# The first adaLN modulation of a two-layer trunk: condition against weights, or weights against condition, on TensorE

## The chip, the core and the metric

The kernel runs on one core of one Trainium2 chip. The metric is device microseconds (us) of one execution, from which medians are taken. The core has five engines with an instruction stream each: TensorE (PE, matrix products, with a separate weight load PEld), VectorE (DVE), ScalarE (ACT), GpSimd (POOL) and SyncE (SP, which here issues most DMAs). Every engine works through its stream in order and waits on semaphores for the others.

## The reference

Two layers over a sequence of 512 tokens of width 1024, in float32. Every sub-layer begins with an RMS norm that is modulated by a shift and a scale, which come from a condition vector c of width 1024:

```python
cond = jax.nn.silu(c)
for layer in range(DEPTH):
    mod = cond @ ada_w[layer] + ada_b[layer]
    shift_m, scale_m, gate_m, shift_f, scale_f, gate_f = jnp.split(mod, N_MOD, axis=-1)
    h = modulate(rms_norm(x, norm_mix_g[layer]), shift_m, scale_m)   # h * (1 + scale) + shift
    ...
    z = h @ ev_w_in[e]           # layer 0: u for S5, then hq, hf, hi, hg for HGRN2
```

Layer 0 is an S5 state space on the 512 channels u beside an HGRN2 recurrence, layer 1 a gated linear attention, and each is followed by a SwiGLU of hidden width 2816. This document is about the start: shift_m and scale_m of layer 0, 2048 numbers, each a sum over 1024 products of cond with a column of ada_w, then h, then the product h @ ev_w_in that gives u.

## The kernel before

Activations stand with channels on the 128 partitions, in eight blocks of 128 channels by 512 tokens (xT[m], and h as a pair hhi, hlo of rounded value and rest, in float32r). A large product is three products of such halves (lines 275 to 277: hi by hi, hi by lo, lo by hi). The helper wsplit makes a weight's halves, ACT the rounded one, DVE the rest.

**The first modulation.** ada_first_loads(half) issues on SP the loads of sixteen weight tiles of 128x512 (256 KB): eight blocks k of the 1024 input channels, for i = 1 (scale) and i = 0 (shift), for half of the output channels. They go into sixteen slots with the tag "s" and one with "n"; a tile of the second half takes the slot of a tile of the first when that has been read. ada_first(half, ws, rows, n) then computes both sums. The scale is done on DVE: acc = acc + w * cond[k] over all 128x512 elements (line 116). The shift is done on PE for the first n blocks, with one column of cond as the weights that stand and the tile of 512 columns passing (line 405), which gives one row of 512 numbers; the rest, for the second half where n = 4, also on DVE (acs). At the end the partitions are summed and turned into columns by products with ones (lines 416 to 421), the bias is added, and gsc, the gain (1 + scale) * norm_mix_g, is formed (line 425). Both halves have their own gsc, and the normed blocks m = 0 to 3 (norm_out, with the tiles ht and hlo) wait for the first, m = 4 to 7 for the second.

**Around it.** s5_params, some 90 small DVE and ACT steps on 128x16 tiles, is put ahead of everything by a priority. x is turned by PE through the identity, four transposes of 128x128 for each block into the PSUM tile xps, and copied by ACT to xT. xn, x times its inverse RMS, is turned likewise into xnps; blocks 4 to 7 are copied to xnT, since they wait longer. Four PSUM tiles rotate under the tag "mm" (xps, xnps 0 to 3, u) and two each under "a" and "b". u has four output blocks q, each of eight input blocks k: u_part does k = 0 to 3, the last loop k = 4 to 7. s5_in_out, s5_mats and s5_tables give POOL its work (B and C matrices, the W products, rotation tables cos and ph).

**What sets the order.** The tile framework schedules the instructions of each engine by its own estimate of time, within dependencies, and fixes the order when the program is built. after(ins) makes what is issued inside it come after ins; "hold" is a POOL copy of gsc that POOL's later work is put behind.

Of the kernel before, what the change touches and what calls it, by code (L numbers as in the profile page):

```python
# [41 lines left out]
def trunk(  # L42
# [22 lines left out]
    def tt(name, tag, shape=(P, T), dtype=F32):  # L65
        return tp.tile(list(shape), dtype, tag=tag, name=name, bufs=SLOTS[tag])
# [4 lines left out]
    def const(name, shape, dtype=F32):  # L71
        return cp.tile(list(shape), dtype, name=name, tag=name)
# [4 lines left out]
    def ps_a(name, shape=(P, T)):  # L77
        return pa.tile(list(shape), F32, tag="a", name=name)
# [6 lines left out]
    def act(o, i, f, **kw):  # L85
        return A.activation(out=o, in_=i, func=f, **kw)  # L86
# [19 lines left out]
    def ttv(e, o, a, b, op):  # L106
        e.tensor_tensor(out=o, in0=a, in1=b, op=op)  # L107

    def tsv(e, o, a, s1, op0, s2=None, op1=None):
        if s2 is None:  # L110
            e.tensor_scalar(out=o, in0=a, scalar1=s1, scalar2=None, op0=op0)
        else:
            e.tensor_scalar(out=o, in0=a, scalar1=s1, scalar2=s2, op0=op0, op1=op1)

    def stt(o, a, s, b, op0, op1):
        V.scalar_tensor_tensor(out=o, in0=a, scalar=s, in1=b, op0=op0, op1=op1)  # L116
# [21 lines left out]

    prow = tt("prow", "s", (16, 4, P))
    nc.scalar.dma_start(out=prow[:, 0, :], in_=s5_lam_re[0].rearrange("(j g) p -> j (g p)", g=2))  # L140
    nc.scalar.dma_start(out=prow[:, 1, :], in_=s5_lam_im[0].rearrange("(j g) p -> j (g p)", g=2))
    lsrow = const("lsrow", [16, 2])
    nc.scalar.dma_start(out=lsrow, in_=s5_log_step[0].rearrange("(j g) -> j g", g=2))
# [211 lines left out]
    def norm_out(xn, parts, q, l, base, m):  # L355

        hh, hl = parts[m]
        gain, shift = gsc[:, q, m : m + 1], mod[:, l, base + m : base + m + 1]
        act(hh, xn, AF.Identity, scale=gain, bias=shift)
        t = tt(f"ht{l}{m}", "t")  # L360
        stt(t, xn, gain, hh.bitcast(F32), ALU.mult, ALU.subtract)
        return V.tensor_scalar(out=hl, in0=t, scalar1=shift, scalar2=None, op0=ALU.add)
# [14 lines left out]
    def ada_first_loads(half):  # L377
        tags = iter("s" * 15 + "n")
        ws = []
        for k in range(KT):  # L380
            for i in (1, 0):
                w = tt(f"ar0{i}{half}{k}", next(tags))
                nc.sync.dma_start(out=w, in_=ada_w[0, k * P : (k + 1) * P, i * D + half * T : i * D + half * T + T])
                ws.append(w)
        return ws
# [4 lines left out]
    def ada_first(half, ws, rows=(), n=KT):  # L390


        acc = tt(f"acc01{half}", "sc")
        acs = tt(f"acc00{half}", "X") if n < KT else None
        fp = ps_a(f"row{half}")
        row = fp[0:1, :]
        last = None
        for k in range(KT):
            c_ = cond[:, k : k + 1]
            if k == 0:  # L400
                tsv(V, acc, ws[0], c_, ALU.mult)
            else:
                stt(acc, ws[2 * k], c_, acc, ALU.mult, ALU.add)
            if k < n:
                ins = PE.matmul(row, lhsT=c_, rhs=ws[2 * k + 1], start=(k == 0), stop=(k == n - 1))
            elif k == n:
                tsv(V, acs, ws[2 * k + 1], c_, ALU.mult)
            else:
                stt(acs, ws[2 * k + 1], c_, acs, ALU.mult, ALU.add)
            if k + 1 in rows:  # L410
                last = rows[k + 1](ins)
        rsb = tt(f"rsb{half}", "sc")[0:1, :]
        act(rsb, row, AF.Copy)
        with after(last):
            for m in range(4):
                PE.matmul(fp[:, m : m + 1], lhsT=acc[:, m * P : (m + 1) * P], rhs=ones[:, 0:1], start=True, stop=True)
            for m in range(4):
                o = fp[:, 4 + m : 5 + m]
                ins = PE.matmul(o, lhsT=rsb[:, m * P : (m + 1) * P], rhs=ones[0:1, 0:1], start=True, stop=acs is None)
                if acs is not None:  # L420
                    ins = PE.matmul(o, lhsT=acs[:, m * P : (m + 1) * P], rhs=ones[:, 0:1], start=False, stop=True)
        for i in range(2):
            c0 = i * 8 + half * 4
            ttv(V, mod[:, 0, c0 : c0 + 4], fp[:, 4 - 4 * i : 8 - 4 * i], cols1[:, c0 : c0 + 4], ALU.add)
        V.scalar_tensor_tensor(
            out=gsc[:, 0, half * 4 : half * 4 + 4], in0=mod[:, 0, 8 + half * 4 : 12 + half * 4], scalar=1.0,
            in1=cols1[:, 96 + half * 4 : 100 + half * 4], op0=ALU.add, op1=ALU.mult)
        return ins
# [139 lines left out]
    def s5_params():  # L568
# [37 lines left out]
        tact(ch, t1, AF.Sin, scale=-0.5, bias=hpic)  # L606
        ttv(V, sb, sh, ch, ALU.mult)
# [41 lines left out]
        return L, cr, ci, rho, fh, fl, pc  # L649
# [272 lines left out]
    with tc.high_priority(offset=-3000):  # L922
        prm = s5_params()
# [5 lines left out]
    aw.append(ada_first_loads(1))  # L929
    raw.append(wraw(us[2], KT, "u2"))  # L930
    crow = tt("crow", "n", (32, 2, P))
# [4 lines left out]
    bcl = s5_in_out_loads()  # L936
    ada_first(0, aw[0])
    hold = G.tensor_copy(out=sm("hold", [P, 4]), in_=gsc[:, 0, 0:4])
# [6 lines left out]
    for m in range(KT):  # L945
        ps = mm_ps(f"xps{m}")
        for b in range(NB):
            PE.transpose(ps[:, b * P : (b + 1) * P], xtok[b][:, m * P : (m + 1) * P], ident)
        act(xT[m], ps, AF.Copy)
    for b in range(NB):  # L950
        if b % 2:
            act(xn[:, b, :], xtok[b], AF.Copy, scale=xrs[:, b : b + 1])
        else:
            tsv(V, xn[:, b, :], xtok[b], xrs[:, b : b + 1], ALU.mult)
    h = norm_parts("m0")
    xns = []
    for m in range(KT):
        ps = (mm_ps if m < 4 else ps_b)(f"xnps{m}")
        for b in range(NB):
            PE.transpose(ps[:, b * P : (b + 1) * P], xn[:, b, m * P : (m + 1) * P], ident)  # L960
        if m < 4:
            hl = norm_out(ps, h, 0, 0, 0, m)
        else:
            xns.append(tt(f"xnT{m}", "t"))
            act(xns[-1], ps, AF.Copy)
    ups = [mm_ps(f"u{q}") for q in range(4)]
    wu = [blocks(wsplit(raw[q], KT, f"u{q}")) for q in range(2)]
# [9 lines left out]
    with after(hl):  # L977
        fold1 = ada_first(1, aw[1], {4: u_part(0, range(4))}, 4)
    raw.append(wraw(us[3], KT, "u3"))
    with after(hl):  # L980
        wu.append(blocks(wsplit(raw[2], KT, "u2")))
    for q in range(1, 3):
        u_part(q, range(4))(None)
    for m in second:
        norm_out(xns[m - 4], h, 0, 0, 0, m)
# [6 lines left out]
    for n in (2, 4):  # L992
        PE.transpose(tps[:, 8 * n : 16 * n], crow[n].rearrange("k g p -> k (g p)"), ident[0 : 8 * n, 0 : 8 * n])
        tact(conds[n], tps[:, 8 * n : 16 * n], AF.Silu)
# [4 lines left out]
    with after(hold):  # L999
        mats = [s5_mats(0)]  # L1000
    with after(G.tensor_copy(out=sm("hold", [P, 4]), in_=gsc[:, 0, 4:8])):
        rot = [s5_tables(q) for q in range(4)]
# [258 lines left out]
```

## Time and profile before

| | us |
|---|---|
| median of 3 runs (1344.96 to 1350.41) | 1345.29 |
| the profiled execution | 1345.65 |
| its span, first to last instruction | 1343.9 |
| PE busy (matmul records) | 1280.0 |
| DVE busy | 766.8 |
| ACT busy | 514.1 |
| POOL busy | 141.4 |

Busy times are of single engines and overlap. A busy PE is not PE at its peak: its level of clock is a separate column (PEclk), and a record lasts longer at the lower level. In a timeline each row is a run of like instructions on one engine: start, duration of the run, line, tiles written and read, shapes, count, and in brackets the idle time before it with what ended it. PE shows two records for one float32 product, and one for a float32r product or a transpose.

### The profile page before, as it was taken

The numbers are of one execution on the slowest core, as the hardware profiler recorded it, in microseconds if no ns is written. First come the engines' busy times: TensorE is split into PE (matmuls) and PEld (weight loads), VectorE is DVE, ScalarE is ACT, GpSimd is POOL, SyncE is SP. The second block draws the span as 40 slices with busy tenths as digits, with TensorE's granted clock in tenths as the row PEclk, the third lists the DMA queues.
The fourth block names the chain that finished last, engine by engine and source line by source line (L and its number), as shares of the span: only waits on it lengthen the run. The fifth ranks groups of instructions, "written<-read, shape, count | busy, mean of one in ns | idle before, by whom it ended". The sixth has DMA issues, their size and how long they took to land.

```text
span 1343.9 us, 18265 instructions
## 1 busy us (share of the span) xinstructions
PE 1280.0 (95%) x6949; PEld 1097.6 (82%) x6949; DVE 766.8 (57%) x1433; ACT 514.1 (38%) x939; POOL 141.4 (11%) x148
## 2 busy tenths in 40 slices
PE   7797999899999999999999999999899999999997
PEld 3577887778888888888888999997888888888886
DVE  5786995787765566566356446657743333333344
ACT  5477358534522222232244433433432222222322
POOL 0593451110100000000010000000100000000000
PEclk9798998999999999999999999999799999999999
DMA  9742531633097669996250322114033323333232
GB/s 305 173 126 79 157 110 38 152 98 102 20 223 189 186 183 230 205 219 185 74 157 21 102 65 78 56 48 133 17 98 103 97 71 99 113 99 104 65 92 79
DMA packets 222824, 159.69 MB, mean 119 GB/s; under 512 B 16752, under 2 KB 195248, under 8 KB 222736
## 3 DMA queue, kind: packets, MB, share of 16 engines
q1 hardware_dynamic: 221696, 157.48, 43.3%
q8 instruction: 54, 0.88, 0.3%
q10 hardware_dynamic: 1040, 1.05, 0.3%
q14 instruction: 34, 0.28, 0.1%
HBM read 156.40 MB, written 2.10 MB: 118 GB/s over the span
## 4 chain that ended last, share of the span: by engine, by line
PE 81%; DVE 10%; ACT 3%; DMA 3%; issue 2%; SPq 0%; POOL 0%; DVEq 0%; ACTq 0%
PE f L275 18%; PE f L276 18%; PE f L277 18%; DMA ar<-in_ada_w_dram 2%; PE op L276 2%; PE lv_g L465 2%; PE op L277 2%; PE op L275 2%; ACT yf L86 1%; PE gr L300 1%; PE gr L301 1%; PE gv L301 1%; PE gr L299 1%; PE gv L300 1%; PE gv L299 1%
## 5 line engine op out<-in xcount | busy, mean ns | idle before, releaser
L276 PE MATMUL f<-hlo_f,whi_f 128*128 128x512 f32 (+1 forms) x736 | 280.8, 383 | 0.4 <-DVE hlo_f L116 0.4
L275 PE MATMUL f<-hhi_f,whi_f 128*128 128x512 f32 (+1 forms) x736 | 279.9, 383 | 0.9 <-ACT hhi_f L86 0.9
L277 PE MATMUL f<-hhi_f,wlo_f 128*128 128x512 f32 (+1 forms) x736 | 280.1, 382 | 0.0
L86 ACT ACTIVATE whi_f<-raw_f 128x1024 fp32r<-128x1024 f32 x88 | 93.3, 1061 | 309.3 <-PE f L276 167.4
L107 DVE TENSOR_TENSOR wlo_f<-raw_f,whi_f 128x1024 fp32r<-128x1024 f32 x88 | 107.7, 1224 | 113.9 <-ACT whi_f L86 113.2
L276 PEld LDWEIGHTS f<-hlo_f,whi_f 128*128 128x128 f32 x736 | 139.2, 189 | 27.2 <-DVE hlo_f L116 1.4
L275 PEld LDWEIGHTS f<-hhi_f,whi_f 128*128 128x128 f32 x736 | 138.9, 190 | 27.5 <-ACT hhi_f L86 1.4
L277 PEld LDWEIGHTS f<-hhi_f,wlo_f 128*128 128x128 f32 x736 | 139.3, 189 | 26.4
L204 DVE SCALAR_TENSOR_TENSOR acc<-ar,cond,acc 128x512 f32<-128x512 f32 x154 | 122.9, 798 | 39.9 <-DMA ar<-in_ada_w_dram 37.8
L277 PE MATMUL f<-hi_g,wlo_c 128*128 128x512 f32 x312 | 121.8, 390 | 0.0
L276 PE MATMUL f<-lo_g,whi_c 128*128 128x512 f32 x312 | 121.7, 390 | 0.0
L275 PE MATMUL f<-hi_g,whi_c 128*128 128x512 f32 x312 | 121.3, 390 | 0.0
L86 ACT ACTIVATE whi_c<-raw_c 128x768 fp32r<-128x768 f32 (+1 forms) x56 | 44.8, 801 | 161.9 <-PE f L276 107.7
L107 DVE TENSOR_TENSOR g<-g,f 128x512 f32<-128x512 f32 x44 | 30.2, 687 | 106.1 <-PE f L277 106.0
L107 DVE TENSOR_TENSOR wlo_c<-raw_c,whi_c 128x768 fp32r<-128x768 f32 (+1 forms) x56 | 50.3, 898 | 60.6 <-ACT whi_c L86 59.1
L275 PEld LDWEIGHTS f<-hi_g,whi_c 128*128 128x128 f32 x312 | 58.6, 188 | 12.1
L276 PEld LDWEIGHTS f<-lo_g,whi_c 128*128 128x128 f32 x312 | 58.6, 188 | 12.1
L277 PEld LDWEIGHTS f<-hi_g,wlo_c 128*128 128x128 f32 x312 | 58.6, 188 | 12.0
L116 DVE SCALAR_TENSOR_TENSOR x<-f,mod,x 128x512 f32<-128x512 f32 (+1 forms) x36 | 24.8, 689 | 40.5 <-PE f L277 40.4
L107 POOL TENSOR_TENSOR na_m<-na_m,nsq_m 128x256 f32<-128x256 f32 x7 | 5.9, 856 | 361.7 <-ACT nsq_m L86 361.7
L300 PE MATMUL gv<-wlo_gv,hhi_m 128*128 128x256 f32 x128 | 36.7, 287 | 0.0
L301 PE MATMUL gv<-whi_gv,hlo_m 128*128 128x256 f32 x128 | 36.6, 287 | 0.0
(668 smaller groups left out, 2651.8 us busy)
## 6 DMA issues: line engine op xcount, KB each, us to landing
raw_f<-in_ffn_w_dram SPq DMA_DIRECT2D x88, 512.0 KB, 4.0
ar<-in_ada_w_dram SPq DMA_DIRECT2D x256, 128.0 KB, 4.2
ar<-in_ada_w_dram SPq DMA_DIRECT2D x64, 256.0 KB, 5.4
raw_c<-in_ffn_w_dram SPq DMA_DIRECT2D x32, 384.0 KB, 3.5
raw_c<-in_ffn_w_dram SPq DMA_DIRECT2D x24, 320.0 KB, 3.2
raw_gv<-in_od_w_in_dram SPq DMA_DIRECT2D x8, 512.0 KB, 3.7
raw_gr<-in_od_w_in_dram SPq DMA_DIRECT2D x8, 512.0 KB, 4.5
raw_o<-in_ev_w_out_dram SPq DMA_DIRECT2D x8, 384.0 KB
```

Of the source, the lines that this page charges most:

```text
L86: return A.activation(out=o, in_=i, func=f, **kw)
L107: e.tensor_tensor(out=o, in0=a, in1=b, op=op)
L116: V.scalar_tensor_tensor(out=o, in0=a, scalar=s, in1=b, op0=op0, op1=op1)
L204: ins = V.scalar_tensor_tensor(out=acc, in0=w, scalar=c_, in1=acc, op0=ALU.mult, op1=ALU.add)
L275: PE.matmul(ps, lhsT=hi, rhs=ah[:, ts], start=(i == 0), stop=False)
L276: PE.matmul(ps, lhsT=hi, rhs=al[:, ts], start=False, stop=False)
L277: ins = PE.matmul(ps, lhsT=lo, rhs=ah[:, ts], start=False, stop=(i == n - 1))
L299: PE.matmul(o, lhsT=ah[:, s], rhs=hi, start=(k == 0), stop=False)
L300: PE.matmul(o, lhsT=ah[:, s], rhs=lo, start=False, stop=False)
L301: PE.matmul(o, lhsT=al[:, s], rhs=hi, start=False, stop=(k == KT - 1))
L465: PE.matmul(ps[0:nk, w, :].rearrange("p (n b) -> p n b", b=b), lhsT=K[:, w * P : w * P + nk], rhs=qv[:, w * nb : (w + 1) * nb, b:], start= ...
```

## The change

ada_first now computes both sums on PE in the other arrangement: a block of 128x128 of the weight tile stands, one column of cond passes, and the 128 sums come out as a column of PSUM, accumulated over k. Per half that is a product of the identity with the bias columns, then 64 products (eight k, two i, four m), one copy to mod and gsc. The DVE sums, the row, its copy (rsb) and the folds with ones go. Between the products, at given k, the argument rows puts other PE work:

```diff
+    def ada_first(half, ws, rows=()):
+        fp = ps_a(f"row{half}")[:, 0:8]
+        m4 = slice(half * 4, half * 4 + 4)
+        bias, mods = (t.rearrange("p (i m) -> p i m", m=8)[:, :, m4] for t in (cols1[:, 0:16], mod[:, 0, 0:16]))
+        f2 = fp.rearrange("p (i m) -> p i m", m=4)
         last = None
+        PE.matmul(fp, lhsT=ident, rhs=bias, start=True, stop=False)
         for k in range(KT):
-            c_ = cond[:, k : k + 1]
-            if k == 0:
-                tsv(V, acc, ws[0], c_, ALU.mult)
-            else:
-                stt(acc, ws[2 * k], c_, acc, ALU.mult, ALU.add)
-            if k < n:
-                ins = PE.matmul(row, lhsT=c_, rhs=ws[2 * k + 1], start=(k == 0), stop=(k == n - 1))
...
+            for i in (1, 0):
+                for m in range(4):
+                    with after(last):
+                        ins = PE.matmul(f2[:, i, m : m + 1], lhsT=ws[2 * k + 1 - i][:, m * P : (m + 1) * P],
+                                        rhs=cond[:, k : k + 1], start=False, stop=(k == KT - 1 and i == 0 and m == 3))
             if k + 1 in rows:
                 last = rows[k + 1](ins)
-        rsb = tt(f"rsb{half}", "sc")[0:1, :]
-        act(rsb, row, AF.Copy)
...
+        V.tensor_copy(out=mods, in_=f2)
...
-    with tc.high_priority(offset=-3000):
-        prm = s5_params()
+    prm = s5_params()
+    next(prm)
...
-    aw.append(ada_first_loads(1))
+    aw.append(ada_first_loads(1, range(4)))
     raw.append(wraw(us[2], KT, "u2"))
+    bcl = s5_in_out_loads()
+    aw[1] += ada_first_loads(1, range(4, KT))
...
+    turn_x(*range(4))(None)
+    last = ada_first(0, aw[0], {4: turn_x(4, 5), 5: turn_x(6, 7), 7: turn_xn(*range(4))})
+    turn_xn(*range(4, KT))(last)
...
+    for m in range(4):
+        with after(hl):
+            hl = norm_out(xnp[m], h, 0, 0, 0, m)[1]
+        if m % 2:
+            with after(hl):
+                wu.append(blocks(wsplit(raw[m // 2], KT, f"u{m // 2}")))
+    with after(hl):
+        prm = next(prm)
...
     with after(hl):
-        fold1 = ada_first(1, aw[1], {4: u_part(0, range(4))}, 4)
+        wu.append(blocks(wsplit(raw[2], KT, "u2")))
+    fold1 = ada_first(1, aw[1], {2 * q + 2: u_part(q, range(4)) for q in range(3)})
...
-    with after(hold):
+    with after(hold), after(ins[0]):
         mats = [s5_mats(0)]
-    with after(G.tensor_copy(out=sm("hold", [P, 4]), in_=gsc[:, 0, 4:8])):
+    with after(G.tensor_copy(out=sm("hold", [P, 4]), in_=gsc[:, 0, 4:8])), after(ins[0]), after(ins[1]):
         rot = [s5_tables(q) for q in range(4)]
```

s5_params has become a generator: its first part, up to the sines, is issued at the start, the rest after the fourth normed block. The log-step row is loaded ahead of the two parameter rows on ACT's queue. In the second half of the program's start, ins is the pair of ACT's and DVE's last steps of normed block 7, which the W products and the tables now come after.

On PE, in the first half, before (row is the PSUM row of the sums, xps the turned x, xnps the turned xn):

```order
L174 MATMUL tps<-cs,rows_91 128x128
L405 MATMUL row_348<-ar_264,cond 1x512
L405 MATMUL row_348<-ar_268,cond 1x512
L948 MATMUL xps_425<-cs,xin 128x128 x4
L948 MATMUL xps_431<-cs,xin 128x128 x4
L405 MATMUL row_348<-ar_272,cond 1x512
L948 MATMUL xps_437<-cs,xin 128x128 x4
L948 MATMUL xps_443<-cs,xin 128x128 x4
L405 MATMUL row_348<-ar_276,cond 1x512
L405 MATMUL row_348<-ar_280,cond 1x512
```

One row product of 512 columns for each block k stands between the transposes. In the same place now:

```order
L403 MATMUL row_340<-cond,ar_218 128x1 x4
L403 MATMUL row_340<-cond,ar_220 128x1 x4
L937 MATMUL xps_374<-cs,xin 128x128 x4
L937 MATMUL xps_380<-cs,xin 128x128 x4
L403 MATMUL row_340<-cond,ar_222 128x1 x4
L403 MATMUL row_340<-cond,ar_224 128x1 x4
L937 MATMUL xps_394<-cs,xin 128x128 x4
L937 MATMUL xps_400<-cs,xin 128x128 x4
L403 MATMUL row_340<-cond,ar_226 128x1 x4
L403 MATMUL row_340<-cond,ar_228 128x1 x4
L403 MATMUL row_340<-cond,ar_230 128x1 x4
L403 MATMUL row_340<-cond,ar_232 128x1 x4
```

Every weight tile, of both sums, has four products of one column; 32 products precede the first of these transposes.

On PE again, ahead of the second gsc, before: the end of the u products of blocks 0 to 3, transposes of the S5 C matrices (cps), and the folds.

```order
L276 MATMUL u_521<-hlo_m_454,whi_u_581 128x512
L277 MATMUL u_521<-hhi_m_453,wlo_u_583 128x512
L679 MATMUL cps_661<-cs,cn 128x128 x4
L679 MATMUL cps_668<-cs,cn 128x128 x4
L416 MATMUL row_533<-ones,acc_531 128x1 x4
L419 MATMUL row_533<-ones,rsb_562 128x1
L421 MATMUL row_533<-ones,acc_532 128x1
```

Now, between the u products of output block 1 and those of output block 2:

```order
L276 MATMUL u_565<-hlo_m_474,whi_u_504 128x512
L277 MATMUL u_565<-hhi_m_474,wlo_u_506 128x512
L403 MATMUL row_572<-cond,ar_268 128x1 x4
L403 MATMUL row_572<-cond,ar_270 128x1 x4
L403 MATMUL row_572<-cond,ar_272 128x1 x4
L403 MATMUL row_572<-cond,ar_274 128x1 x4
L275 MATMUL u_566<-hhi_m_474,whi_u_568 128x512
L276 MATMUL u_566<-hlo_m_475,whi_u_568 128x512
```

The second half's sums, which were DVE's and then folded after all of u's first half, now stand on PE in runs of sixteen products behind each u block; the last run ends ahead of the second gsc.

On ACT, from the copies of x blocks 4 to 7 (x_145 to x_148) to the first normed block, before:

```order
L86 ACTIVATE x_147<-xps_437 128x512
L86 ACTIVATE x_148<-xps_443 128x512
L86 ACTIVATE s5s<-pc 128x16 x2
L86 ACTIVATE lbm<-lbm 128x4 x3
L101 ACT_TABLE_LOAD
L86 ACTIVATE whi_u_523<-raw_u_294 128x1024
```

and now:

```order
L86 ACTIVATE whi_u_492<-raw_u_238 128x1024
L86 ACTIVATE whi_u_504<-raw_u_240 128x1024
L86 ACTIVATE x_145<-xps_374 128x512
L86 ACTIVATE x_146<-xps_380 128x512
L86 ACTIVATE whi_u_568<-raw_u_258 128x1024
L86 ACTIVATE x_147<-xps_394 128x512
L86 ACTIVATE x_148<-xps_400 128x512
L86 ACTIVATE hhi_m_474<-xnps_422,mod,gsc 128x512
```

The rounding of the u weights, u2's among it, has moved ahead of the last copies of x.

## Rows read from the trace of the kernel before

**Rows 1.** The page, busy tenths and granted clock in 40 slices of the span.

```profile
PE   7797999899999999999999999999899999999997
...
PEclk9798998999999999999999999999799999999999
```

**Rows 2.** Stretches: length, busy PE, PEld, DVE, ACT, POOL (instructions), PEclk, DMA share, GB/s.

```profile
5.50:11.40 5.90, 5.54 (x20) 3.44 (x20) 0.82 (x6) 3.82 (x7) 0.00 (x0) 1.00 0.85 288
...
21.20:34.40 13.20, 13.20 (x67) 6.33 (x66) 11.27 (x64) 8.41 (x19) 0.00 (x0) 1.00 1.09 360
34.40:51.90 17.50, 13.84 (x59) 8.81 (x57) 17.33 (x44) 8.24 (x16) 6.64 (x9) 1.00 0.97 241
51.90:65.10 13.20, 9.00 (x33) 7.66 (x33) 6.12 (x9) 5.38 (x10) 12.87 (x19) 0.50 0.45 98
65.10:69.00 3.90, 3.89 (x9) 3.12 (x10) 3.90 (x8) 2.40 (x6) 1.42 (x1) 0.51 0.02 4
```

**Rows 3.** Timeline of DVE: start, us, line, tiles, count, idle before.

```profile
13.44 0.49 DVE L111 TENSOR_SCALAR acc<-ar,cond 128x512 f32<-128x512 f32 x1 [4.78 <-DMA ar<-in_ada_w_dram]
...
34.18 0.17 DVE L425 SCALAR_TENSOR_TENSOR gsc<-mod,cols 128x4 f32<-128x4 f32 x1
...
51.70 2.20 DVE L116 SCALAR_TENSOR_TENSOR acc<-ar,cond,acc 128x512 f32<-128x512 f32 x2
...
60.22 0.17 DVE L425 SCALAR_TENSOR_TENSOR gsc<-mod,cols 128x4 f32<-128x4 f32 x1
...
67.43 0.48 DVE L362 TENSOR_SCALAR hlo_m<-ht,mod 128x512 fp32r<-128x512 f32 x1
...
96.98 0.69 DVE L107 TENSOR_TENSOR rz0a<-vps,cos 128x512 f32<-128x512 f32 x1
```

**Rows 4.** Timeline of PE up to 34 us, columns as before.

```profile
14.18 1.87 PE L405 MATMUL row<-ar,cond 128*1 128x512 f32 x2 [2.81 <-DMA ar<-in_ada_w_dram]
...
18.75 1.97 PE L948 MATMUL xps<-cs,xin 128*128 128x128 f32 x8
...
21.83 1.10 PE L948 MATMUL xps<-cs,xin 128*128 128x128 f32 x8
...
30.83 1.02 PE L405 MATMUL row<-ar,cond 128*1 128x512 f32 x2
...
31.78 1.05 PE L416 MATMUL row<-ones,acc 128*128 128x1 f32 x8
```

**Rows 5.** Timeline of PE from 53 to 106 us.

```profile
53.95 1.87 PE L416 MATMUL row<-ones,acc 128*128 128x1 f32 x8 [4.36 <-DVE acc L116]
...
59.33 0.59 PE L421 MATMUL row<-ones,acc 128*128 128x1 f32 x2
...
61.36 1.65 PE L275 MATMUL u<-hhi_m,whi_u 128*128 128x512 f32 x3
...
105.65 0.58 PE L300 MATMUL hv<-wlo_hv,hhi_m 128*128 128x256 f32 x1 [4.61 <-DVE wlo_hv L107]
```

**Rows 6.** The chain that ended last, in order of time: start, us, what.

```profile
31.85 0.98 PE row L416 x8
...
65.11 0.80 PE u L276
...
66.76 0.43 PE u L276
...
69.20 0.23 PE u L276
```

**Rows 7.** DVE's sums by the tile ar: count, min/median/max ns, first and last start.

```profile
L116 DVE SCALAR_TENSOR_TENSOR acc<-ar,cond,acc x17: 730/751/1220, 16.3 to 52.9; 128x512 f32<-128x512 f32 x17
```

**Rows 8.** Timeline of POOL, the first step of the rotation tables.

```profile
61.15 1.04 POOL L107 TENSOR_TENSOR ph<-s5s,cidx 128x512 f32<-128x512 f32 x1
```

**Rows 9.** Timeline of SP, the loads of u0 and u1.

```profile
20.31 1.33 SPq L243 DMA_DIRECT2D raw_u<-in_ev_w_in_dram  x2
```

**Rows 10.** By the tile raw_u: from issue to landing.

```profile
DMA to landing us min/median/max: 6.6/6.9/7.3
```

## What the change does to the time: a prediction

> **What bounds the kernel now.** The page's slices come first [rows 1]: they show TensorE (PE) at nine tenths or more in nearly all slices after the fourth. What the front of the program gains or loses before 134 us is therefore passed on to the end almost whole. So I read the front by stretches [rows 2], then in time.
>
> The front has two hinges, the moments when the gains of a half of the first modulation are ready: gsc at 34.18 + 0.17 = 34.35 us and at 60.22 + 0.17 = 60.39 us [rows 3]. Before the first, PE multiplies rows of the condition into the weights (L405), turns x and xn, and folds the sums (L416, L419) [rows 4]. Before the second, PE stands idle for 4.36 us until VectorE (DVE) has summed the second half's weights, 2.20 us for the last two with GpSimd (POOL) beside it [rows 3, 5]. DVE is busy for 17.33 of the 17.5 us there [rows 2]. Then the folds run, the second normed blocks follow, and from 65.11 us the u products run densely [rows 6].
>
> The second thing to see is the clock. From 51.9 to 65.1 us PE was granted 0.50 [rows 2]. There four folds (eight records) took 1.87 us; at 31.78 us they took 1.05 [rows 4, 5]. The same halving stands before 21 us: eight transposes took 1.97 us at 18.75 and 1.10 at 21.83, two L405 records 1.87 at 14.18 and 1.02 at 30.83 [rows 4]. The page's PEclk digit is 9 there [rows 1], but the durations are those of the lower level, 1.2 of 2.4 GHz: until about 21 us PE ran slowly.
>
> **The price of one new product.** A new product has weights of 128x128 f32 standing and one column of the condition passing. That is the form of L416: 128*128, 128x1 f32 [rows 4, 5]. Four of those, eight records, took 0.98 us in the chain at the upper level, 0.245 us each [rows 6]; at 0.50, 1.87/4, about 0.465 us [rows 5]. Sixteen weight tiles of four products are 64 per half. Twelve row products, the folds and the 20 sums on DVE (0.75 us alone, up to 1.22 beside POOL [rows 7]) go.
>
> **At which level do they run?** The decision lies here. In 53.95 to 59.9 us PE was filled with one-column folds [rows 5], and the level stayed at 0.50; so it did through three 512-column products at 61.36. It rose only after u had run from 65.1 to about 69: u products are 0.43 us apart at 66.76, 0.23 at 69.20 [rows 5, 6]. Twenty records, nearly all transposes, filled 5.54 of the 5.9 us before 11.4 [rows 2], still at the slow pace of 0.28 us each, without a rise either. What did come just before the rise at 21 us were L405 records of 512 columns with transposes between, and these are what the change removes. I take the lower level for the whole first half.
>
> **First half.** It can start when the first weights land, at 13.44 us, where DVE's first sum waited for them [rows 3]. The condition and the bias are there earlier. 64 x 0.465 = 29.8 us. PE's order puts 32 transposes in between (x blocks 4 to 7, xn blocks 0 to 3): 32 x 1.97/8 = 7.9 us. 13.4 + 29.8 + 7.9 = 51.1, where the last fold ended before at 33.8: 17 us later. One copy and gsc follow, as now in about 0.5: first gains at 51.6. A tile lasts 1.86 us on PE, so no load holds this up.
>
> **Second half.** PE next has 16 xn transposes (3.9) and 16 products (7.4), up to 62.5 us. ScalarE (ACT) and DVE make the first four normed blocks and split the weights beneath it: the second four took 7.5 us before (60.39 to 67.91 [rows 3]), and two weight splits go between, each over twice the elements of a 0.75 us step [rows 7], so 3 more and about 62. That cover is thin, but PE is last. Then three runs of 12 u products alternate with three of 16 modulation products. All low: 36 x 0.43 + 48 x 0.465 = 37.8, ending at 100.3. All high: 36 x 0.23 + 48 x 0.245 = 20.1, ending at 82.6. Runs of u raised the clock before and one-column runs did not, so I take the middle, 91.4, and second gains at 91.9: 31.5 us later than before (22.5 to 40.4).
>
> **After it.** The normed blocks no longer share with POOL, whose rotation tables now wait for the last of them: u started 4.7 us after the gains before, 65.11 less 60.39 [rows 3, 6], and DVE's two-input steps cost 1.22 instead of 0.75 us beside POOL [rows 7]. I take 2 us back. More is possible, since a split that PE waited 4.61 us for at 105.65 [rows 5] now stands ahead of the rotation steps: at best 6 back. At worst 3 more: the tables started at 61.15, one us after the gains [rows 8], and now start some 5 later with the W products beside them; their cover is the first use, at 96.98, 36 us after the gains [rows 3]. If it fails, DVE waits.
>
> Costed at nothing: the S5 parameters, moved behind the first normed blocks, end before POOL needs them since PE is still on products (uncovered, their some 35 small DVE steps delay the gains by a few us). The six loads for B and C now precede twelve of the second half's weights on SP's queue; together 0.75 MB, 2 us at 360 GB/s [rows 2], and PE asks for those weights after 62 us. The split of u2 moved ahead of two x copies on ACT; under a slow PE it is done first. The u3 load on SP waits for the first split, and the loads for hq and hf behind it; all have 30 us.
>
> **Sum.** The profiled execution took 1345.65 us (span 1343.9), the median is 1345.29: the same. 1345.65 + 31.5 - 2 = 1375. The forecast's own range is 1345.65 + 22.5 - 6 = 1362 to 1345.65 + 40.4 + 3 = 1389.
>
> **Rivals.**
> 1. *The clock rises midway in the first half*, say at the 16 xn transposes, and stays. The first half then saves some 7 us, and the rest runs as all high: 44 + 20 + 6 = 70.5 for the second gains, 10 late, 2 back: 1354. For: the transposes were among what ran before the rise at 21 us. Against: alone they did not raise it.
> 2. *Dense products raise the clock as at 21 us and hold it.* Then 16 products run slowly to 21, 48 take 11.8 us, 32 transposes 4.4: 37 us. A second wait ends there too: x block 7's copy stands behind the split of u2 on ACT. u0 and u1 are issued at 20.31 [rows 9] and land 6.9 us later [rows 10]; four tiles and u2, 1.6 MB at 360 GB/s, bring u2 to about 32, the copies to 34.4, and the last transposes and eight products to 37. Then 16 transposes 2.2, 64 products 15.7 and 36 u 8.3: 63.5, gains at 64.0, 3.6 late; 2 back: 1347. For: at 31.78 the folds ran at the upper level without losing it [rows 4]. Against: 5.9 us of them did not raise it [rows 5].
> The Trainium skill (TensorE: Matmul & The Clock Gate, Part 1) says that the default state is throttled and sustained activity releases the throttle; by that, 15 us of unbroken products would give this rival's 1347. Its Part 4 says transposes do not count as busy in the same way, which the slow transposes before 11.4 us agree with; the folds at 53.95 are the row against the first rule.
> 3. *Faster: a product costs one record, not two*, because the next weights load beside it: 0.1225 us at the upper level. It decides from about 0.23 us per product and passes 0.5% at 0.13. The first gains stay at 36 (u2's landing), the second come at 36.5 + 2.2 + 8.3 + 7.8 = 55, 5 early, 2 back: 1338. Against: in L416 loads and products already overlapped.
>
> **Chances.** Forecast 0.72, rival 1 0.12, rival 2 0.10, rival 3 0.06. The range reaches from below rival 1, 1351, to 1387, and leaves out rivals 2 and 3 and the forecast's last tail, about 0.18. One measurement can tell 0.5%, 6.7 us, from no change: faster 0.06, same 0.11 (rival 2 and the edge of rival 1), slower 0.83.
>
> **What would show it.** Right: first gsc near 51 us, second between 83 and 101; L403 records 0.23 us apart for most of the first half; PE busy yet at the transposes' and products' slow durations from 13 to 60 us; DVE idle there. Wrong: L403 records 0.12 apart by 25 us and first gains before 40 (rivals 2 and 3), or a second half that POOL or the tables end and not PE.

## The result, and the profile after

The changed kernel took **1382.08 us** (median of 4 runs, 1379.18 to 1382.66) against 1345.12 for the kernel before beside it: ratio **1.0262**, 95% interval 1.0232 to 1.0291, slower. The forecast was 1375 (1351 to 1387), so the sign and the range held. The profiled execution took 1382.26 us, 36.6 more than the profiled one before, and the sum of the prediction missed it by 7.3 us. Inside the sum the two terms up to the second gains were together 3.9 us too large, and the one for what follows them had the wrong sign and was 11.0 too small; the experiments are about both. Single executions that took far longer than their neighbours (3244.08 us in the second experiment) are left out of all ratios.

The page first: busy time, share of the span and instructions of PE, and the two slice lines that answer to [rows 1].

```profile
PE 1318.3 (95%) x7145; PEld 1148.0 (83%) x7145; DVE 757.2 (55%) x1411; ACT 511.9 (37%) x937; POOL 135.1 (10%) x148
...
PE   7999989779999999999999999999899999999997
...
PEclk9979989979999999999999999999999999999999
```

PE was busy 38.3 us longer (1280.0 before) in a span 36.6 us longer. Its waits together are the same as before within 2 us (63.9 and 62.2), so over the whole span the loss is PE's longer work, not waiting. But the waits moved, as the stretches show (length, busy PE, PEld, DVE, ACT, POOL, PEclk, DMA share, GB/s; the first four answer to [rows 2]).

```profile
21.20:34.40 13.20, 13.20 (x64) 13.20 (x64) 0.00 (x0) 3.69 (x5) 0.00 (x0) 1.00 1.01 275
34.40:51.90 17.50, 17.50 (x86) 17.50 (x84) 1.08 (x3) 4.68 (x9) 0.19 (x1) 1.00 0.77 219
51.90:65.10 13.20, 11.52 (x43) 9.86 (x43) 6.16 (x10) 1.81 (x4) 0.00 (x0) 1.00 0.14 40
65.10:69.00 3.90, 3.90 (x27) 3.62 (x26) 3.62 (x24) 0.00 (x0) 0.00 (x0) 1.00 0.62 175
260.00:310.00 50.00, 35.11 (x202) 31.12 (x201) 40.00 (x99) 24.26 (x57) 10.35 (x7) 0.83 0.43 111
```

Between 34.4 and 65.1 us PE idled 7.9 us before and idles 1.7 now. Further on stands a hole: 14.9 us idle at 260 to 310 us, around glu, the gate product over the four S5 quarters, which begins at 293.45. In the kernel before glu begins at 255.71, and the 50 us that stand alike to it have 5.7 us idle, 9.1 less:

```profile
222.30:272.30 50.00, 44.25 (x270) 39.23 (x269) 41.47 (x86) 29.13 (x65) 13.63 (x7) 0.93 0.51 127
```

The hinges, in DVE's timeline, answer to [rows 3]: first gsc at 48.64 us (34.35 before, forecast 51.6), second at 87.98 (60.39 before, forecast 91.9).

```profile
48.48 0.16 DVE L408 SCALAR_TENSOR_TENSOR gsc<-mod,cols 128x4 f32<-128x4 f32 x1
...
58.83 0.49 DVE L362 TENSOR_SCALAR hlo_m<-ht,mod 128x512 fp32r<-128x512 f32 x1 [8.51 <-PE xnps L937]
...
87.82 0.16 DVE L408 SCALAR_TENSOR_TENSOR gsc<-mod,cols 128x4 f32<-128x4 f32 x1
```

PE's timeline, answering to [rows 4, 5]. Two records are one product of L403, and four products use up one weight tile.

```profile
14.29 13.79 PE L403 MATMUL row<-cond,ar 128*128 128x1 f32 x64
...
34.69 6.83 PE L403 MATMUL row<-cond,ar 128*128 128x1 f32 x32
41.38 3.65 PE L937 MATMUL xnps<-cs,xn 128*128 128x128 f32 x16
44.83 3.41 PE L403 MATMUL row<-cond,ar 128*128 128x1 f32 x16
...
61.69 0.80 PE L277 MATMUL u<-hhi_m,wlo_u 128*128 128x512 f32 x1 [1.52 <-DVE wlo_u L107]
62.28 0.63 PE L275 MATMUL u<-hhi_m,whi_u 128*128 128x512 f32 x1
62.71 0.63 PE L276 MATMUL u<-hlo_m,whi_u 128*128 128x512 f32 x1
...
66.12 4.00 PE L403 MATMUL row<-cond,ar 128*128 128x1 f32 x32
...
74.40 4.34 PE L403 MATMUL row<-cond,ar 128*128 128x1 f32 x32
...
83.87 3.71 PE L403 MATMUL row<-cond,ar 128*128 128x1 f32 x32
```

In this profile the whole first half runs at the lower level: 13.79/32 = 0.43 us for each product at the start, 6.83/16 = 0.43 at 35 us and 3.41/8 = 0.43 at 45, and sixteen transposes take 3.65 us. PE is busy without a gap from 14 to 58 us and the level doesn't rise. (The clock column reads 1.00 there all the same; the last section comes back to that.) It rises when u has run: the u products of 62 to 66 us stand 0.43 us apart, and the sixteen products after them take 4.00 us, 0.25 each; the u products behind those are 0.43 apart again at first (70.71 to 72.42). The same happens around the products of 74 and 84 us. All 128 products together:

```profile
L403 PE MATMUL row<-cond,ar 128*128 128x1 f32 x256 | 46.5, 315 | 0.0
```

Of the kernel before, the row products went (its group below) and the folds, 2.0 us in the first half and 6.0 in the second [rows 4, 5]: 21.7 us.

```profile
L405 PE MATMUL row<-ar,cond 128*1 128x512 f32 x24 | 13.7, 675 | 3.7 <-DMA ar<-in_ada_w_dram 3.7
```

So 25 of the 38.3 us are the products themselves. Up to the second gains PE was busy 45.15 us before and is 78.52 now, 33.4 more: beside the 25 some 7 are the 36 u products of that stretch, now 0.43 us apart where they were 0.23 apart (39.81 to 48.31 us). The last 4.9 us lie behind the second gains, where the work is nearly the same (6777 records of PE instead of 6766) and took longer.

### The profile page after: what moved, and what is told of

It reads as the page before. It is cut to its first block, busy times and chain, and to the rows that moved or that the text cites. A ratio compares the mean times of both kernels' runs of the same rounds, so it can differ in the third digit from the quotient of the medians.

```text
span 1380.5 us, 18624 instructions
## 1 busy us (share of the span) xinstructions
PE 1318.3 (95%) x7145; PEld 1148.0 (83%) x7145; DVE 757.2 (55%) x1411; ACT 511.9 (37%) x937; POOL 135.1 (10%) x148
## 4 chain that ended last, share of the span: by engine, by line
PE 83%; DVE 7%; ACT 5%; DMA 3%; issue 1%; POOL 0%; SPq 0%; DVEq 0%; ACTq 0%; POOLq 0%
PE f L275 18%; PE f L276 17%; PE f L277 17%; PE row L403 3%; PE op L275 2%; PE op L276 2%; PE op L277 2%; PE lv_g L448 2%; DMA ar<-in_ada_w_dram 1%; ACT yf L86 1%; PE gr L300 1%; PE gr L301 1%; PE gr L299 1%; PE gv L301 1%; PE gv L300 1%
## 5 line engine op out<-in xcount | busy, mean ns | idle before, releaser
L403 PEld LDWEIGHTS row<-cond,ar 128*128 128x128 f32 x256 | 47.5, 287 | 0.5
L403 PE MATMUL row<-cond,ar 128*128 128x1 f32 x256 | 46.5, 315 | 0.0
```

The source lines that it names most:

```text
L403: ins = PE.matmul(f2[:, i, m : m + 1], lhsT=ws[2 * k + 1 - i][:, m * P : (m + 1) * P], rhs=cond[:, k : k + 1], start=False, stop=(k == KT ...
```

## The experiments

Theory A is that of the prediction: PE's one-column products at the lower level set both gains, and what comes later there is passed on. Beside it stood the question of the last term: why the second gains were 27.6 us late and the end 36.6.

### One half, the other half, both

ada_sums is ada_first of the kernel before under another name (its lines are left out here); the placing of transposes, S5 parameters and rotation tables stays the changed one.

```diff
# first experiment
-    last = ada_first(0, aw[0], {4: turn_x(4, 5), 5: turn_x(6, 7), 7: turn_xn(*range(4))})
+    last = ada_sums(0, aw[0], {4: turn_x(4, 5), 5: turn_x(6, 7), 7: turn_xn(*range(4))})
# second experiment
-    fold1 = ada_first(1, aw[1], {2 * q + 2: u_part(q, range(4)) for q in range(3)})
+    with after(hl):
+        fold1 = ada_sums(1, aw[1], {4: u_part(0, range(4))}, 4)
+    for q in range(1, 3):
+        u_part(q, range(4))(None)
# third experiment: both
```

> Changed kernel, but the first half is formed as before (VectorE sums, eight L405 rows, folds; the transposes stay placed between the rows); the second half is still 64 products. Theory A (TensorE's products set both gains, and a gain that comes later is passed on whole): first gsc at 34 to 37 us instead of 48.6, the second some 39 later as now, near 75 instead of 88, time 1382 - 13 = 1369 us. Rival B (the second half waits for its own weights or for VectorE, not for the first gains): second gsc at 82 or later, time 1376 or more.

> Changed kernel, but the second half is formed as before (four rows on TensorE, twelve sums on VectorE, folds); the first half is still 64 products. Theory A: first gsc at 48.6 as now, the second 26 us later as in the kernel before (34.35 to 60.39), near 74.7 instead of 88, time 1382 - 13 = 1369 us. Rival B (the second half costs what it costs only through the low clock, and the sums leave the clock low too): second gsc 82 or later, time 1376 or more.

> Both halves formed as before; what is left of the change is the placing of transposes, S5 parameters, S5 matrices and rotation tables (behind the second normed blocks). Theory A (the tables behind the second normed blocks cost 9 us after the second gains, whatever set those gains): gsc at about 34.5 and 60.5, time 1345 + 9 = 1354 us. Rival B (the 9 us arise only when the gains are late): 1345 us, no change against the kernel before. Rival C (the products cost the whole 37 us and the placing gains): under 1343.

Measured: **1358.90 us**, ratio to before 1.0088 (1.0073 to 1.0103), for the first half by sums; ratio **1.0164** (1.0132 to 1.0195), some 1369 us, for the second; **1352.19 us**, ratio 1.0040 (1.0027 to 1.0053), for both. The gains of the first and of the third, in DVE's timelines:

```profile
32.19 0.16 DVE L448 SCALAR_TENSOR_TENSOR gsc<-mod,cols 128x4 f32<-128x4 f32 x1
67.97 0.16 DVE L408 SCALAR_TENSOR_TENSOR gsc<-mod,cols 128x4 f32<-128x4 f32 x1
```

```profile
30.83 0.16 DVE L448 SCALAR_TENSOR_TENSOR gsc<-mod,cols 128x4 f32<-128x4 f32 x1
...
60.78 0.15 DVE L448 SCALAR_TENSOR_TENSOR gsc<-mod,cols 128x4 f32<-128x4 f32 x1
```

Undoing the first half moves the second gains by 20 us (87.98 to 68.13), more than the 13 forecast, and the time by 23; undoing the second moves them by 7 and the time by 13; undoing both, by 27 and 30. So theory A holds for the larger part, and rival B falls in the first experiment. It came near in the second: the time was theory A's 1369, but the gains were at 80.8, not 74.7. DVE's sums began at 64.09 us there, behind normed blocks and splits that were late themselves. What is left with both halves undone, 5 us with an interval of 3.6 to 7.1, is the price of the placing alone: some of theory A's 9 us, more than rival B's nothing. Rival C, that the placing gains, falls.

### The rotation tables

```diff
-    with after(hl):
-        prm = next(prm)
+    prm = next(prm)            # at the start, behind the first next(prm)
-    with after(hold), after(ins[0]):
+    with after(hold):
         mats = [s5_mats(0)]
-    with after(G.tensor_copy(out=sm("hold", [P, 4]), in_=gsc[:, 0, 4:8])), after(ins[0]), after(ins[1]):
+    with after(hold):
         rot = [s5_tables(q) for q in range(4)]
```

> Changed kernel, but the S5 parameters are made wholly at the start and the rotation tables and S5 matrices are held back by the first gains alone, no longer by the second normed blocks. Theory A (GpSimd's tables and W products are what is late after the second gains): second gsc near 88 as now, last table step before 95 instead of 122.5, time 1382 - 9 = 1373 us or less. Rival B (the tail's loss has another cause, such as the low clock at 121 to 128 us): 1380 to 1384.

Measured: **1378.27 us**, ratio 1.0235 (1.0218 to 1.0252). That is inside what the changed kernel itself gave in two sets of runs (1376.16 to 1383.61). The tables did move. POOL's timeline in this experiment has its last table step at 77.59, and then waits for the C matrix that ACT copies (s5c):

```profile
77.59 1.33 POOL L107 TENSOR_TENSOR ph<-ph,cos 128x512 f32<-128x512 f32 x1
91.92 1.17 POOL L107 TENSOR_TENSOR W0a<-s5c,s5L 128x256 f32<-128x256 f32 x1 [13.00 <-ACT s5c L86]
```

In the changed kernel the tables begin at 88.19 and POOL comes to the next quarter's matrices only at 122.47:

```profile
88.19 2.48 POOL L107 TENSOR_TENSOR ph<-s5s,cidx 128x512 f32<-128x512 f32 x2
...
122.47 1.83 POOL L107 TENSOR_TENSOR B1a<-s5b,s5L 128x256 f32<-128x256 f32 x2
```

With the tables done 43 us earlier (78.9 instead of 122.5) the first use of them came 11 us earlier (rz0a at 119.9 instead of 130.9), but glu began at 291.3 instead of 293.5. Theory A falls: the tables are late, and the 9 us are not theirs; the medians give them 1 to 4 us at most, within the spread.

### The last S5 quarter

The hole at 260 to 310 us ends with the first glu product, after a wait of 8 us:

```profile
293.45 0.79 PE L275 MATMUL glu<-hi_yr,whi_wg 128*128 128x512 f32 x1 [7.96 <-ACT hk L86]
```

The copy hk that it names stands in ACT's order behind the 16 yf copies of the last quarter (282.40 to 288.83), so that quarter ends the wait. Followed back, it starts late. (In each quarter vps is the product of the inputs U with the weights wn, yp a product later on that gives the output, and yf its copy.) Its weights wn are copied by ACT at 245.18 and 253.99, behind the yf copies of the third quarter; in the kernel before the first of the two stood ahead of these (200.92, with yf at 206.00) and the second behind them, at 214.53. Nothing in the change's text touches these lines. The scheduler, which orders by its estimate of time, put them elsewhere. The fifth experiment only gives them a priority:

```diff
         for i in range(2):
+            with tc.high_priority(offset=400) if q == 3 else nullcontext():
                 ps = ps_b(f"wnp{q}{i}", (P, 4, P))
                 ...
                 act(w, ps, AF.Copy)
```

> Changed kernel; only the transposes and copies wnp and wn of the last S5 quarter stand earlier on TensorE and ScalarE, ahead of the yf copies of the third quarter, as they do in the kernel before. Theory A (the place of these copies on ScalarE is what makes the fourth quarter 40 us late instead of 31): vps of the last quarter starts near 248 us instead of 256.7, glu near 285 instead of 293.5, time 1382 - 6 = 1376 us, since the u and hg products fill part of the wait. Rival B (what is gained there is waited for elsewhere): 1380 to 1384.

Measured: **1370.64 us** (1369.14 to 1373.12), ratio 1.0173 (1.0152 to 1.0194). ACT's timelines, the changed kernel first, then the experiment:

```profile
236.67 6.36 ACT L86 ACTIVATE yf<-yp 32x128 f32<-32x128 f32 x16
...
245.18 0.60 ACT L86 ACTIVATE wn<-wnp 128x512 f32<-128x512 f32 x1
...
253.99 0.58 ACT L86 ACTIVATE wn<-wnp 128x512 f32<-128x512 f32 x1
```

```profile
225.99 0.60 ACT L86 ACTIVATE wn<-wnp 128x512 f32<-128x512 f32 x1 [9.48 <-PE wnp L727]
...
230.15 4.37 ACT L86 ACTIVATE yf<-yp 32x128 f32<-32x128 f32 x11
234.53 0.60 ACT L86 ACTIVATE wn<-wnp 128x512 f32<-128x512 f32 x1
```

The last quarter's vps starts at 241.6 instead of 256.7, glu at 278.2 instead of 293.5, and PE's idle time in the 50 us around glu falls from 14.9 to 8.2 (244.80 to 294.80). But not all of the 11.4 us between the medians belong to wn: in this profile the second gains stood at 83.7, 4.3 earlier, though the instructions up to there are the same in the same order. So the changed kernel was profiled again.

> The changed kernel itself, beside the eleventh, since the fifth had its second gains 4.3 us earlier than the changed kernel's profile though the code up to there is the same. Theory A (the level's changes fall at other moments from one execution to the next, and move the second gains by some us): second gsc between 83 and 88, time 1375 to 1383 us, so of the fifth's 11.5 us only 7 belong to wn. Rival B (they are the same each time): 88.0, 1380 to 1383 us.

Measured: **1379.21 us** (1376.16 to 1383.61), second gains at 88.01, as in the first profile, so rival B holds for the gains, and the fifth's profile is the one that differs. The runs spread over 7 us; the two profiles agree within 2. Between the medians of the fifth experiment and this one lie 8.6 us. Measured from the second gains the lead of the front drops out: up to glu it is 194.5 us in the fifth experiment against 205.5 and 203.9 in the two profiles of the changed kernel, and 195.3 in the kernel before. From the second gains to the end of the span the rows are, for the kernel before, the changed kernel and the fifth experiment:

```profile
60.39:1343.90 1283.51, 1234.83 (x6766) 1070.81 (x6765) 729.60 (x1300) 486.44 (x886) 124.91 (x104) 0.98 0.42 112
87.98:1380.50 1292.52, 1239.77 (x6777) 1075.62 (x6776) 730.00 (x1299) 488.13 (x894) 124.94 (x111) 0.97 0.41 112
83.69:1367.20 1283.51, 1234.21 (x6777) 1068.91 (x6776) 732.52 (x1300) 488.32 (x894) 125.97 (x111) 0.98 0.41 112
```

So in the profiles all 9.0 us behind the second gains are gone with wn early, 3.5 of them waits of PE and 5.6 its records. The mechanism, the place of wn, is shown in the trace. Its price by the medians is 4 to 7 us (8.6 and 11.4, less the front's 4.3), if all executions of the fifth had that lead, which only the profiled one shows.

The same edit on the third experiment and on the kernel before:

> Both halves by sums as in the third experiment, and the last quarter's wnp and wn early as in the fifth. Theory A (what the placing costs is the late wn of the last S5 quarter, and nothing else): 1352 - 11 = 1341 us, glu from 268 to about 257, so level with the kernel before or 4 us faster (first gsc at 31 instead of 34.35). Rival B (the placing costs its 7 us in the rotation tables held behind the second normed blocks): 1348 us or more.

> Kernel before; only the last S5 quarter's wnp and wn stand earlier. There the first wn is already ahead of the yf copies and the second stood 13 us behind it (200.9 and 214.5). Theory A (the S5 chain up to glu sets the end): vps of the last quarter starts near 212 instead of 217.1, glu near 251 instead of 255.7, time 1341 us. Rival B (in the kernel before the chain waits for something else by then): 1344 to 1347 us.

Measured: **1351.88 us**, ratio 1.0033 (1.0019 to 1.0047), against 1.0040 without it; and **1348.22 us**, ratio 1.0004 (0.9987 to 1.0021). In the first, glu moved from 268.0 to 256.5 us in the profiles, and PE's wait for it went:

```profile
268.05 0.80 PE L275 MATMUL glu<-hi_yr,whi_wg 128*128 128x512 f32 x1 [9.48 <-ACT hk L86]
```

```profile
256.48 0.50 PE L275 MATMUL glu<-hi_yr,whi_wg 128*128 128x512 f32 x1 [0.70 <-ACT hk L86]
```

But the median did not follow; the profiled execution, 1347.91, was among the fastest of twelve. In the second, glu stayed (255.7 and 257.3): there it had waited 2.75 us for DVE's hq, not for ACT. Theory A misses both. So a late wn makes PE wait before glu, which two pairs of profiles show (7.96 and, in the fifth experiment, 0.93 us; 9.48 and 0.70); that the time follows, only the fifth experiment shows, and the 5 us of the placing have a cause that these runs don't name.

### What holds the clock

```diff
+        if half == 0:
+            dm = tt("dm", "sc", dtype=F32R)
+            act(dm, xtok[0][:, 0:T], AF.Copy)
+            dps = ps_b("dense")
         for k in range(KT):
             for i in (1, 0):
+                for _ in range(4 if half == 0 else 0):
+                    with after(last):
+                        PE.matmul(dps, lhsT=dm[:, 0:P], rhs=dm, start=True, stop=True)
                 for m in range(4):
```

> Changed kernel with added work that nobody reads: before each of the 16 weight tiles of the first half four products of 512 columns (x rounded to fp32r), 64 in all; the first 16 of them stand together before the fourth tile's last product. Theory A (dense products raise the clock and hold it, one-column products alone lose it): L403's products fall from 0.43 to 0.23 us after the first dozen dense ones, the dense ones cost 0.23, and the first gsc comes at 48 to 52 us, hardly later than now (48.6) though 64 products are added; time 1380 to 1388. Rival B (the level stays low whatever runs here): 64 x 0.43 = 27.5 us more, first gsc at 76, time about 1409.

Measured: **1379.03 us**, ratio 1.0229 (1.0206 to 1.0253): 64 products that nobody reads were added in front, and the time is that of the changed kernel. PE's timeline of this experiment (L410 is L403's line here):

```profile
14.67 6.54 PE L410 MATMUL row<-cond,ar 128*128 128x1 f32 x30
21.07 6.18 PE L407 MATMUL dense<-dm 128*128 128x512 f32 x16
...
27.24 1.17 PE L407 MATMUL dense<-dm 128*128 128x512 f32 x4
28.25 0.95 PE L410 MATMUL row<-cond,ar 128*128 128x1 f32 x8
...
49.80 0.95 PE L410 MATMUL row<-cond,ar 128*128 128x1 f32 x8
```

Fifteen products take 6.54 us (0.43 each); then sixteen dense ones run, and from there four products take 0.95 us (0.23 each, some of it overlap) until 52 us. The first gains come at 52.96, 4.3 later than without the added work, and the second at 88.35, where it was 87.98. Theory A holds, rival B falls. Fewer dense products, put ahead, were to show a gain (dm is made by DVE at the start here; the diff is against the changed kernel):

```diff
+        if half == 0:
+            dps = ps_b("dense")
+            for _ in range(12):
+                PE.matmul(dps, lhsT=dm[:, 0:P], rhs=dm, start=True, stop=True)
         for k in range(KT):
             for i in (1, 0):
+                for _ in range(2 if half == 0 else 0):
+                    with after(last):
+                        PE.matmul(dps, lhsT=dm[:, 0:P], rhs=dm, start=True, stop=True)
...
+    V.tensor_copy(out=dm, in_=xtok[0][:, 0:T])
```

> Changed kernel with 44 products of 512 columns that nobody reads in the first half: twelve, and those of the first five tiles, run before the first weights are used (x rounded by VectorE at the start), then two stand before each further tile. Theory A (the low level is what the first half costs more than its columns): products at 0.23 instead of 0.43 us from the start of the half or soon after, 14.6 for the 64, 4.4 for the transposes, some 22 dense ones at 0.23, first gsc near 41 instead of 48.6, time 1382 - 7 = 1375 us. Rival B (two dense products of 0.23 to four of one column don't hold the level): products at 0.43 again before 30 us, first gsc at 50 or later, 1382 us or more.

Measured: **1393.01 us**, ratio 1.0339 (1.0317 to 1.0362). The order placed 22 dense products ahead, and the level rose and was lost again:

```profile
17.72 2.11 PE L407 MATMUL dense<-dm 128*128 128x512 f32 x8
...
19.81 4.79 PE L410 MATMUL row<-cond,ar 128*128 128x1 f32 x40
24.46 1.20 PE L407 MATMUL dense<-dm 128*128 128x512 f32 x2
25.46 1.70 PE L410 MATMUL row<-cond,ar 128*128 128x1 f32 x8
...
49.15 1.70 PE L410 MATMUL row<-cond,ar 128*128 128x1 f32 x8
...
54.92 0.95 PE L410 MATMUL row<-cond,ar 128*128 128x1 f32 x8
```

The twenty products at 19.81 ran at 0.24 us, and after them four take 1.70 (0.43 each) up to 50 us, in spite of two dense ones between. Then sixteen transposes ran at the lower level, and behind them, with two dense ones between as before, four products took 0.95 again. So two dense ones neither held the level from 25 to 50 us nor kept it from rising later; why it rose then, no run shows. Rival B holds: here the added products are pure cost, first gains at 57.6, second at 98.5.

### Sums and products together

Both start from the kernel before, which left PE idle while DVE summed. Two experiments give PE the last four of the sixteen weight tiles of the second half as sixteen one-column products, so that DVE has eight sums there instead of twelve; the second also runs the folds ahead of the u1 and u2 products, and wn early (left out of the diff).

```diff
-        for k in range(KT):
+        for k in range(pk):                # pk = 6 in the second half
 ...
+            for k in range(pk, KT):
+                for i in (1, 0):
+                    for m in range(4):
+                        PE.matmul(f2[:, i, m : m + 1], lhsT=ws[2 * k + 1 - i][:, m * P : (m + 1) * P],
+                                  rhs=cond[:, k : k + 1], start=False, stop=False)
 ...
-        u_part(q, range(4))(None)          # second of the two only
+        u_part(q, range(4))(fold1)
```

> Kernel before, with one thing of the change: in the second half the last four of the sixteen weight tiles go through TensorE as sixteen one-column products in the gap where it waited for VectorE, so VectorE has eight sums instead of twelve. Theory A (VectorE's sums end last there): four sums of about 1 us less, second gsc near 57.5 instead of 60.4, time 1345.3 - 3 = 1342 us. Rival B (16 products at the low level, 0.43 us each or 6.9 us, and the folds behind them take the place of the sums): second gsc 60 to 62, time 1345 to 1348.

> The seventh experiment (last four weight tiles of the second half as products) with the folds ahead of the u1 and u2 products on TensorE, since VectorE's sums were there done at 51.4 while the folds began at 55.4; and the last quarter's wnp and wn early. Theory A (each us of the second gains and of the last quarter reaches the end): second gsc near 54, time 1356 - 4 - 11 = 1341 us or less. Rival B (gains before 60 us don't help, the first S5 quarter waits for GpSimd's products and the tables): 1345 us or more.

Measured: **1355.95 us**, ratio 1.0061 (1.0045 to 1.0077), second gains at 58.1; and **1346.20 us**, ratio **0.9982** (0.9971 to 0.9992), second gains at 54.3:

```profile
54.15 0.16 DVE L434 SCALAR_TENSOR_TENSOR gsc<-mod,cols 128x4 f32<-128x4 f32 x1
```

The gains came as forecast in both, 2 and 6 us earlier, and the time did not follow: 8 us slower the first time, which neither of its theories had, and 2.4 faster, not 6, the second, which is rival B's time. In the first, the vps of the first and last quarter are late (98.3 and 231.4; 89.9 and 217.1 before). In the second, the u1 and u2 products only moved from before the gains to behind them, and PE finished its first hq block at 91.4 where it was 92.8. That these are the reasons wasn't tested. This last kernel is the one that beats both, by 0.18% against the kernel before.

## Why the prediction was right, and where its sum was wrong

**The level.** Right for the changed kernel, and it carried the forecast. The folds at 0.50 [rows 2, 5] were the row to trust: in both profiles of the changed kernel one-column products and transposes did not raise the level in 44 us of unbroken work, and such products did not hold it after u had raised it. The Trainium skill (TensorE: Matmul & The Clock Gate, Part 1) says that activity releases the throttle. Here PE was busy for 13.20 of 13.20 and 17.50 of 17.50 us at the lower level, so the trace speaks against the rule as it stands there. The sixth and the eleventh experiment show that it matters what PE is busy with. Rival 2 fell with that. Rival 1 fell by its time, but not its place: in the fourth and fifth experiments, with the same products and transposes in front, the level did rise behind the 16 xn transposes and was lost again within 8 us. The row of the fourth, eight products at 0.23 us each:

```profile
45.27 1.84 PE L403 MATMUL row<-cond,ar 128*128 128x1 f32 x16
```

The first gains came at 47.51 and 46.06 there, 1.1 and 2.6 us before the changed kernel's, where rival 1, with a level that stays, had 7. Rival 3 fell too: a product is two records of 0.215 us.

**The first half** was 3 us too long: 51.6 against 48.64. The term that was mis-sized is the price, 0.465 us from 1.87/4 [rows 5]. From start to start the 64 products took 26.9 us, 0.42 each, instead of 29.8, and the 32 transposes 6.9 instead of 7.9; the start was 0.9 later (14.29 for 13.4).

**The second half** came out at 87.98 for 91.9, with the lateness of the first half in it. From first to second gains it took 39.3 us, 40.3 forecast. The price again made the 1 us: the 16 transposes and 16 products before u took 10.3 us, not 11.4. From u on the middle between all low and all high was right to 0.2 us, and that is in part luck. The prediction did not say which work would have which level: the products ran at 0.25 us and u mostly at 0.43, 27.4 us together, and 1.7 us of waits that it did not count made up the middle. The thin cover is where they came from. The first hlo was not made until 58.83, behind the last xnps transposes that DVE waited 8.51 us for, and PE waited 0.15 us for it and 1.52 us for wlo_u.

**After it** is the step of the sum that failed. The prediction took 2 us back (6 back to 3 more) and named the tables and W products as what could be late, with a cover of 36 us. Measured: 36.6 - 27.6 = 9.0 us more, outside its bounds. Right behind the gains it was right in part: u followed them by 3.7 us, not 4.7. The tables began 0.2 us after the gains (88.19), not some 5 later, but W products ran between them, and counted from the gains their first use came 6.3 us later than before (130.85 and 96.98). That cost nothing that the fourth experiment could take back. What cost was further on, in a stretch that the prediction never looked at: the S5 quarters are a chain, and at its end PE stood idle. From the second gains to glu the changed kernel took 205.5 us for 195.3. Two copies on ACT, which the scheduler had moved, stood behind others there; with them early the fifth experiment's profile has 194.5 us to glu and the kernel before's 1283.5 us to the end. By the medians that is 4 to 7 of the 9 us; in the eighth experiment the same edit took the wait away and not the time, so the rest stays open.

**Costed at nothing.** The S5 parameters: POOL waited 21.35 us for them until 70.24, but had finished B0 at 80, before the second gains; nothing of the second gains was lost there. The loads: PE's timeline has no wait of L403 for its weights once the products have begun. The sum of the placing, though, wasn't nothing: 5 us with both halves undone.

## What to carry to other kernels

Before PE takes over reductions as one-column products, price them from rows of that very shape at the lower clock, and ask which work beside them would hold the clock. A chain that is hidden under PE's other work has its price at the end, where that work runs out: read the stretch in which the chain is awaited, not only the one that the edit touches. Where a scheduler sets the order, compare the order of all engines far behind the edit, since it moves copies there that no line of the change names.

## What the chip showed that was not expected

- In the changed kernel one-column products left PE at the lower level, 1.2 of 2.4 GHz, and lost the upper one when it was there: 0.43 us for each from 14 to 58 us without an idle moment, 0.25 as a mean behind u, and u back at 0.43 after each sixteen, three times.
- Four products of 512 columns before each four of one column kept the upper level for 25 us (0.95 us for four). Two of them did not from 25 to 50 us (1.70 us), though behind sixteen transposes the level was up again beside two (0.95 at 54.92).
- The clock column can read 1.00 over a stretch at the lower level. In the changed kernel 14 to 58 us reads 1.00; the fifth experiment, the same products with the same 3.41 us for eight at 28 us, reads 0.59 for this stretch:

```profile
13.80:48.00 34.20, 33.76 (x183) 33.59 (x183) 6.90 (x39) 14.02 (x29) 0.19 (x1) 0.59 0.96 277
```

- The moments at which the level changes aren't fixed by the code. In the fifth experiment two runs of products, at 14.10 and 43.62, were at the upper level for a while, and the first gains came at 46.06; two profiles of the changed kernel, with the same code up to there, had 48.64 and 48.65.
